# Three more seven-product blocks in the down projection of half 1, their weights loaded by rows, two banks seeded earlier, x reloaded after the last weight

## The chip, the cores and the metric

The kernel runs on 1 core of one Trainium2 chip. The metric is device time in microseconds (us); the kernel before takes 1061.85 us, the median of 3 runs (1061.6 to 1062.74). A core has TensorE (PE in the profile, with its weight load PEld), VectorE (DVE), ScalarE (ACT), GpSimd (POOL) and SyncE (SP), which here only issues DMAs. Each engine works through its own instructions in their order and waits where an operand, or the room for its result, isn't there yet.

## The reference, cut to what matters

One decoder layer on 256 tokens with 2048 channels, in float32. The part that the change touches is the end of its channel mixer:

```
u = causal_dwconv(h @ w_up, conv_w, conv_b)          # 256 x 11264
gate, val = split(u, 2)
y = (gelu(gate) * val) @ w_down                      # (256 x 5632) @ (5632 x 2048)
x = x + rmsnorm(y, post_ffn_g)
```

Attention, the input and output projections and the up projection come ahead of it and are computed as before.

## The kernel before, in words

**Products in float32.** Every weight is split into a high part (fp32r, by ACT: `whi`) and the rest (by DVE: `wlo = raw - whi`), and every activation likewise. A product is then three matmuls, high by high, high by low and low by high, into one PSUM bank (`products`, L973). A unit of weights is 128 partitions x 1024 numbers, 512 KB: SP loads it into one of 5 `raw` buffers (L72), ACT writes one of 5 `whi` buffers, DVE one of 5 `wlo` buffers.

**The down projection** runs in two halves of the 5632 rows. A half holds 22 row tiles of 128 in `G[0]` to `G[21]`, 256 tokens in two tiles t = 0 and 1, and makes two column pairs: n = 0 (columns 0 to 1023) and n = 2 (columns 1024 to 2047). For two row tiles, `four` (L1024) makes the products of one 512-column block with both tokens' tiles: 4 products of 512 columns, 12 matmuls. Two calls make the 8 products of a 2 x 2 x 2 block (row tiles x column blocks x token tiles).

**`seven`** (L988) makes those 8 products with 7, by Winograd's form of Strassen's scheme. Tokens' sums s1 to s4 come from POOL (L946 to L949) and are split into `sums`; weights' sums are made by DVE in place in the raw buffers (L1002 to L1005) and split as well. Of the 7 products, a, b and e (9 matmuls) come first, and d, f, c and g (12 matmuls, `others`, L1010) after the `four` calls of the same step, so that DVE has time for the sums. Seven splits of 512 columns and 4 subtractions are needed. The products a, c, d and f gather in four "att" banks over all sevens of the pair, and `fold` (L1031) then adds them to the four result blocks of y_sb: one ACT copy and 8 DVE additions in half 1. The table SEVENS (L28) says in which steps of a pair a seven stands: in half 0 at steps 0, 1, 3 and 4 of both pairs, in half 1 at steps 0, 2 and 4 of pair n = 0 and nowhere in pair n = 2.

**The last pair (half 1, n = 2; "the tail")** is made otherwise. The loop L1060 makes column block 2 alone (12 matmuls a step), and then L1115 makes column block 3: token tile 0 into bank e (6 matmuls of 512 columns for two row tiles), token tile 1 into two banks b1 in halves of 256 columns (12 matmuls of 256). For the last 6 pairs of row tiles (HOLD) the products of token tile 1 are put off to the end (`held`), so that token tile 0 can be normalised while PE still works. The banks b1 don't start from zero: at L1111 to L1114 a matmul opens each, and ACT copies into it what y_sb already holds for that block. PE's next product into b1 waits for this copy.

**Around it.** At a pair's end `down` (L963) adds a bank to y_sb (DVE), sums its squares (ACT, L967) and multiplies with post_ffn_g (POOL); for pair n = 0 of half 1 the four multiplications are listed in `gains` and are issued in the tail's loop (L1074). At the very end `finish` (L1105) multiplies with the reciprocal norm, adds x and stores. x was put aside in `x_dram`; it comes back into `x_end` (L1131), in the buffer in which `sums` stood. PE's order is the order of the code; the orders of DVE, ACT, POOL and SP are set by a scheduler when the kernel is built.

## Time and profile before

The profiled execution took 1063.41 us by the same clock as the runs and has a span of 1061.7 us; the runs without a profile have a median of 1061.85 us. A profile's busy time of an engine is the time in which an instruction of it runs; instructions of one engine overlap a little, so a group's count times its mean can be more.

| stretch of the trace (us from the start) | what runs | length | PE busy | DVE busy | ACT busy | POOL busy |
|---|---|---|---|---|---|---|
| 577.4 to 634.6 | half 0, pair 0 (four sevens) | 57.2 | 57.20 | 49.75 | 32.88 | 1.69 |
| 634.6 to 691.7 | half 0, pair 2 (four sevens) | 57.1 | 57.04 | 48.77 | 31.43 | 0.00 |
| 932.7 to 990.6 | half 1, pair 0 (three sevens) | 57.9 | 57.90 | 48.59 | 32.88 | 2.47 |
| 990.6 to 1020.5 | tail, column block 2 | 29.9 | 29.90 | 16.94 | 14.87 | 6.67 |
| 1020.5 to 1036.9 | tail, column block 3, both token tiles | 16.4 | 14.99 | 9.47 | 7.29 | 3.55 |
| 1036.9 to 1045.1 | tail, token tile 0 alone | 8.2 | 8.20 | 0.00 | 0.00 | 0.00 |
| 1045.1 to 1061.7 | held products, norm, stores | 16.6 | 8.62 | 7.51 | 1.67 | 2.35 |

In a row of a timeline the columns are the start, the duration, the engine, the line, the operation, result<-operands, shapes and count, and in brackets the engine's idle time ahead of it with what ended it.

### The profile page before, as it was taken

The numbers are of one execution on the slowest core, as the hardware profiler recorded it, in microseconds if no ns is written. First come the engines' busy times: TensorE is split into PE (matmuls) and PEld (weight loads), VectorE is DVE, ScalarE is ACT, GpSimd is POOL, SyncE is SP. The second block draws the span as 40 slices with busy tenths as digits, with TensorE's granted clock in tenths as the row PEclk, the third lists the DMA queues.
The fourth block names the chain that finished last, engine by engine and source line by source line (L and its number), as shares of the span: only waits on it lengthen the run. The fifth ranks groups of instructions, "written<-read, shape, count | busy, mean of one in ns | idle before, by whom it ended". The sixth has DMA issues, their size and how long they took to land.

```text
span 1061.7 us, 16409 instructions
## 1 busy us (share of the span) xinstructions
PE 1050.2 (99%) x5941; PEld 914.6 (86%) x5941; DVE 803.8 (76%) x1330; ACT 634.0 (60%) x1119; POOL 252.1 (24%) x278
## 2 busy tenths in 40 slices
PE   9999999999999999999999999999999999999996
PEld 7889988888889888888888888888888888888886
DVE  5989877876468787777768888868786777787653
ACT  6767766677557666655556555556565556555450
POOL 4253235441122433312111000013321212100210
PEclk9999999999999999999999999999999999999999
DMA  8645665555875766666664666866576656557742
GB/s 279 204 120 169 179 204 189 180 158 160 297 237 178 226 201 197 200 189 201 185 195 139 209 207 196 251 194 192 179 211 192 193 181 199 175 162 267 270 154 80
DMA packets 165550, 207.10 MB, mean 195 GB/s; under 512 B 6844, under 2 KB 131036, under 8 KB 164444
## 3 DMA queue, kind: packets, MB, share of 16 engines
q1 hardware_dynamic: 165148, 205.65, 61.9%
q8 instruction: 47, 0.77, 0.3%
q10 hardware_dynamic: 320, 0.40, 0.1%
q14 instruction: 35, 0.29, 0.1%
HBM read 201.68 MB, written 4.21 MB: 194 GB/s over the span
## 4 chain that ended last, share of the span: by engine, by line
PE 90%; DVE 4%; DMA 2%; issue 2%; ACT 1%; POOL 0%; SPq 0%; DVEq 0%; POOLq 0%; ACTq 0%
PE bank_acc L262 21%; PE bank_att L262 15%; PE bank_acc L975 13%; PE bank_acc L284 13%; PE bank_acc L269 11%; PE bank_att L269 8%; DMA raw<-in_w_down_dram 2%; PE bank_att L975 2%; DVE wlo L121 1%; PE bank_att L450 1%; PE bank_att L485 1%; PE bank_att L494 1%; DVE wlo L288 1%; PE bank_att L225 1%; PE bank_acc L881 1%
## 5 line engine op out<-in xcount | busy, mean ns | idle before, releaser
L121 DVE TENSOR_TENSOR wlo<-raw,whi 128x1024 fp32r<-128x1024 f32 (+3 forms) x335 | 408.7, 1233 | 140.4 <-ACT whi L118 133.5
L118 ACT CAST whi<-raw 128x1024 fp32r<-128x1024 f32 (+3 forms) x334 | 340.8, 1035 | 196.7 <-issue 90.7
L262 PE MATMUL bank_acc<-hT,whi 128*128 128x512 f32 x1024 | 245.6, 392 | 0.0
L262 PEld LDWEIGHTS bank_acc<-hT,whi 128*128 128x128 f32 x1024 | 188.2, 188 | 37.1
L857 POOL TENSOR_TENSOR u<-u,rowf 128x256 f32<-128x256 f32 x88 | 94.5, 1095 | 447.3 <-DVE u L856 444.3
L975 PE MATMUL bank_acc<-whi,G 128*128 128x512 f32 x520 | 167.6, 389 | 0.1
L262 PE MATMUL bank_att<-hT,whi 128*128 128x512 f32 x704 | 165.7, 390 | 0.0
L262 PEld LDWEIGHTS bank_att<-hT,whi 128*128 128x128 f32 x704 | 130.6, 188 | 26.2
L269 PEld LDWEIGHTS bank_acc<-hT,wlo 128*128 128x128 f32 x1024 | 123.5, 188 | 3.2
L269 PE MATMUL bank_acc<-hT,wlo 128*128 128x256 f32 x1024 | 125.8, 278 | 0.0
L975 PEld LDWEIGHTS bank_acc<-whi,G 128*128 128x128 f32 x520 | 97.6, 188 | 20.3 <-DVE y_sb L965 0.5
L975 PE MATMUL bank_acc<-wlo,G 128*128 128x512 f32 x260 | 101.2, 389 | 0.0
L269 PEld LDWEIGHTS bank_att<-hT,wlo 128*128 128x128 f32 x704 | 83.6, 188 | 1.9
L269 PE MATMUL bank_att<-hT,wlo 128*128 128x256 f32 x704 | 83.9, 277 | 0.0
L284 PE MATMUL bank_acc<-whi,oT 128*128 128x512 f32 (+1 forms) x272 | 81.8, 379 | 0.0
L287 ACT CAST whi<-raw 128x512 fp32r<-128x512 f32 x77 | 44.4, 621 | 27.2 <-DMA raw<-in_w_down_dram 14.5
L288 DVE TENSOR_TENSOR wlo<-raw,whi 128x512 fp32r<-128x512 f32 x77 | 52.7, 727 | 9.9 <-ACT whi L287 9.8
L284 PEld LDWEIGHTS bank_acc<-whi,oT 128*128 128x128 f32 x272 | 50.2, 188 | 9.3
L975 PEld LDWEIGHTS bank_acc<-wlo,G 128*128 128x128 f32 x260 | 48.8, 188 | 9.8
L284 PE MATMUL bank_acc<-wlo,oT 128*128 128x512 f32 (+1 forms) x136 | 51.2, 377 | 0.0
L284 PE MATMUL bank_acc<-whi,hT 128*128 128x384 f32 (+1 forms) x192 | 46.9, 323 | 0.0
L859 ACT ACTIVATE yg<-u,cw 128x256 f32<-128x256 f32 x44 | 26.5, 603 | 33.7 <-POOL u L857 33.7
(250 smaller groups left out, 1284.4 us busy)
## 6 DMA issues: line engine op xcount, KB each, us to landing
raw<-in_w_up_dram SPq DMA_DIRECT2D x176, 512.0 KB, 4.5
raw<-in_w_down_dram SPq DMA_DIRECT2D x88, 512.0 KB, 4.9
raw<-in_w_in_dram SPq DMA_DIRECT2D x51, 512.0 KB, 4.9
raw<-in_w_out_dram SPq DMA_DIRECT2D x32, 512.0 KB, 4.7
raw<-in_w_in_dram SPq DMA_DIRECT2D x16, 384.0 KB, 3.3
cb<-c_dram SPq DMA_DIRECT2D x8, 256.0 KB, 4.2
x_sb<-in_x_dram SPq DMA_DIRECT2D x2, 1024.0 KB, 6.0
x_dram<-x_sb SPq DMA_DIRECT2D x2, 1024.0 KB, 5.9
```

Source lines behind the costliest of these rows:

```text
L118: i1 = act.copy(hi[:, cs], raw[:, cs])
L121: i2 = dve.tensor_tensor(lo[:, cs], raw[:, cs], hi[:, cs].bitcast(F32), op=ALU.subtract)
L225: pe.matmul(b, hi[:, a, m * P:(m + 1) * P], hT[:, kt, 0:512], start=(kt == 0), stop=(kt == KT - 1))
L262: pe.matmul(b, hi[:, a, m * P:(m + 1) * P], hT[:, kt, 0:512], start=(kt == 0), stop=(last == (0, kt)))
L269: pe.matmul(b[:, 256:512], lo[:, a, m * P:(m + 1) * P], hT[:, u * 4 + a, 0:256], start=False, stop=(last == (1, u * 4 + a)))
L284: pe.matmul(b, a, r[:, cols], start=(first and i == 0), stop=(last and i == 2))
L287: act.copy(hi, src)
L288: dve.tensor_tensor(lo, src, hi.bitcast(F32), op=ALU.subtract)
L450: pe.matmul(sb[e][:, cs], a[r, t * P:(t + 1) * P], b[r, 0:nk], start=(n == 0), stop=(n == 2))
L857: pool.tensor_tensor(u[:, 2:258], u[:, 2:258], rowf, op=ALU.mult)
L859: act.activation(y, u[:, 2:258], AF.Identity, bias=cw[:, 3, ch:ch + 1], scale=cw[:, 2, ch:ch + 1])
L975: pe.matmul(b, x, r, start=b not in opened and not i, stop=closes and i == 2)
```

## The change

1. SEVENS for half 1 becomes (0, 1, 3, 4) in pair 0, so a fourth seven, and (0, 2) in the tail, which had none. The tail's loop then has 9 steps instead of 11, and the loop of column block 3 starts at the third pair of row tiles.
2. `seven` loads its weights by rows: two loads of 128 x 1024 (row tiles k and k + 1, both column blocks) instead of two of 2 x 128 x 512 (one column block each). `split_into` replaces `split_512`: the splits are one of 512 columns and three of 1024 instead of seven of 512. This holds for all sevens, half 0 too.
3. The banks b1 are opened and filled in the tail's loop, after step 6 (two steps before its end), instead of behind it.
4. The two reloads of x stay at their place in the program, which is behind the last weight's load; before, the scheduler put them among the weights. Their buffer is that of `sums`, which the tail now reads in its step 2.

```diff
-SEVENS = (((0, 1, 3, 4), (0, 1, 3, 4)), ((0, 2, 4), ()))
+SEVENS = (((0, 1, 3, 4), (0, 1, 3, 4)), ((0, 1, 3, 4), (0, 2)))
...
-            def split_512(dst, i, src):
-                cs = slice(i * 512, i * 512 + 512)
-                hi, lo = dst[0][:, cs], dst[1][:, cs]
-                split(hi, lo, src)
-                return hi, lo
+            def split_into(dst, src, n):
+                hi, lo = (x[:, :n * 512] for x in dst)
+                split(hi, lo, src[:, :n * 512])
+                return [(hi[:, i:i + 512], lo[:, i:i + 512]) for i in range(0, n * 512, 512)]
...
-                left, right = [w_load(w_rows(w_down, k, 2, m * 512, 512), 2, 512)[0]
-                               for m in (n, n + 1)]
-                b11, b21, b12, b22 = (x[:, i * 512:i * 512 + 512] for x in (left, right)
-                                      for i in range(2))
+                top, low = [w_load(w_rows(w_down, k + i, 1, n * 512, 1024), 1, 1024)[0]
+                            for i in range(2)]
+                b11, b12, b21, b22 = (x[:, i:i + 512] for x in (top, low) for i in (0, 512))
...
-                dst = w_parts(UNIT, held=False)
-                w11 = split_512(dst, 0, b11)
-                w22 = split_512(dst, 1, b22)
-                w21 = split_512(w_parts(UNIT, held=False), 0, b21)
+                (w11,) = split_into(w_parts(UNIT, held=False), top, 1)
+                w21, w22 = split_into(w_parts(UNIT, held=False), low, 2)
...
-                    dst = w_parts(UNIT, held=False)
-                    t1 = split_512(dst, 0, b11)
-                    t3 = split_512(dst, 1, b12)
-                    dst = w_parts(UNIT, held=False)
-                    t2 = split_512(dst, 0, b22)
-                    t4 = split_512(dst, 1, b21)
+                    t1, t3 = split_into(w_parts(UNIT, held=False), top, 2)
+                    t4, t2 = split_into(w_parts(UNIT, held=False), low, 2)
...
+                    if tail and i == (at[-1] + 4 if at else 0):
+                        b1 = [bank("att"), bank("att")]
+                        for x, cs in zip(b1, halves):
+                            pe.matmul(x[:, cs], G[0][:, 0:P], G[0][:, 0:256], start=True,
+                                      stop=False)
+                            act.copy(x[:, cs], y_sb[:, 1, 1536:2048][:, cs])
...
-        b1 = [bank("att"), bank("att")]
-        for x, cs in zip(b1, halves):
-            pe.matmul(x[:, cs], G[0][:, 0:P], G[0][:, 0:256], start=True, stop=False)
-            act.copy(x[:, cs], y_sb[:, 1, 1536:2048][:, cs])
...
-            sp.dma_start(x_sb[:, t, :], x_dram[t * P:(t + 1) * P, :])
+            i = sp.dma_start(x_sb[:, t, :], x_dram[t * P:(t + 1) * P, :])
+            if at:
+                tc.keep_in_program_order(i)
```

**Three places of the new order.** On DVE, at the passage from pair 0 of half 1 to the tail, the kernel before has this piece. `bank_acc` with L965 is a `down`, L121 the low part of a `four`'s weights:

```order
L1051 TENSOR_TENSOR y_sb<-y_sb,s 128x512
L121 TENSOR_TENSOR wlo<-raw,whi 128x1024 x2
L965 TENSOR_TENSOR y_sb<-bank_acc,y_sb 128x512 x2
L121 TENSOR_TENSOR wlo<-raw,whi 128x1024
L965 TENSOR_TENSOR y_sb<-bank_acc,y_sb 128x512 x2
L121 TENSOR_TENSOR wlo<-raw,whi 128x1024 x10
```

The changed kernel has this at the same place, where L998 to L1001 are the subtractions of a seven and L288 its low parts:

```order
L965 TENSOR_TENSOR y_sb<-bank_acc,y_sb 128x512 x2
L1000 TENSOR_TENSOR raw<-raw 128x512
L121 TENSOR_TENSOR wlo<-raw,whi 128x1024
L965 TENSOR_TENSOR y_sb<-bank_acc,y_sb 128x512 x2
L1001 TENSOR_TENSOR raw<-raw 128x512
L288 TENSOR_TENSOR wlo<-raw,whi 128x1024 x2
L121 TENSOR_TENSOR wlo<-raw,whi 128x1024
L288 TENSOR_TENSOR wlo<-raw,whi 128x512
```

The tail's first low part of a `four` now stands behind the first two `down` additions, and the two low parts of `others` (the pair of L288 rows) behind all four.

On PE, the kernel before opens the banks b1 (L1113) between the last product of column block 2 and the first of column block 3 (`G_7487` and `G_7488` are the last two row tiles of the half, `G_7467` the first):

```order
L975 MATMUL bank_acc<-whi,G_7488 128x512 x2
L975 MATMUL bank_acc<-wlo,G_7488 128x512
L975 MATMUL bank_acc<-whi,G_7488 128x512
L1113 MATMUL bank_att<-G_7467 128x256 x2
L975 MATMUL bank_acc<-whi,G_7467 128x512
L975 MATMUL bank_acc<-wlo,G_7467 128x512
L975 MATMUL bank_acc<-whi,G_7467 128x512
L284 MATMUL bank_att<-whi,G_7467 128x256
```

In the changed kernel the same two matmuls are L1070 and stand behind the row tiles 16 and 17 of the half (`G_7435` and `G_7436`):

```order
L975 MATMUL bank_acc<-whi,G_7436 128x512 x2
L975 MATMUL bank_acc<-wlo,G_7436 128x512
L975 MATMUL bank_acc<-whi,G_7436 128x512
L1070 MATMUL bank_att<-G_7419 128x256 x2
L975 MATMUL bank_acc<-whi,G_7437 128x512
L975 MATMUL bank_acc<-wlo,G_7437 128x512
```

Between the opening and the first product into b1 (L284) there are now 24 matmuls of column block 2, for row tiles 18 to 21, and 3 into bank e, where only those 3 stood.

On SP, the end of the changed kernel's queue reads:

```order
L72 DMA raw<-in_w_down_dram 128x1024 x2
L72 DMA raw<-in_w_down_dram 128x2x512 x2
L72 DMA raw<-in_w_down_dram 128x1024 x2
L72 DMA raw<-in_w_down_dram 128x2x512 x16
L1125 DMA x_end<-x_dram 128x2048 x2
L1106 DMA out_dram<-y_sb 128x512 x6
```

Both reloads of x (L1125) stand behind all weights; before, 21 and 15 weights were behind the first and the second.

## The prediction

> **What bounds the kernel now.** I read the page first, then busy time by stretches, then the chain of waits at the end of the span, then the timelines of the engines there. From the page:
>
> ```profile
> PE 1050.2 (99%) x5941; PEld 914.6 (86%) x5941; DVE 803.8 (76%) x1330; ACT 634.0 (60%) x1119; POOL 252.1 (24%) x278
> PE   9999999999999999999999999999999999999996
> PEclk9999999999999999999999999999999999999999
> ```
>
> PE is busy for all but the last slice, at its full clock. So a matmul that goes away is time that goes away, as long as the other engines keep ahead of PE; and the only other thing to win is a gap in PE's row. The stretches of the down projection (us, then PE, PEld, DVE, ACT, POOL with counts, clock, DMA share, GB/s):
>
> ```profile
> 577.40:634.60 57.20, 57.20 (x254) 47.36 (x253) 49.75 (x73) 32.88 (x49) 1.69 (x2) 1.00 0.60 195
> 932.70:990.60 57.90, 57.90 (x258) 47.92 (x257) 48.59 (x66) 32.88 (x47) 2.47 (x3) 1.00 0.69 229
> 990.60:1020.50 29.90, 29.90 (x133) 24.76 (x132) 16.94 (x15) 14.87 (x17) 6.67 (x4) 1.00 0.72 242
> 1020.50:1036.90 16.40, 14.99 (x94) 13.13 (x93) 9.47 (x10) 7.29 (x12) 3.55 (x2) 1.00 0.30 106
> ```
>
> The first row is a pair with four sevens, the second the pair with three, then the tail's column block 2 and the part of column block 3 with both token tiles. PE has a gap in the last one only, where the banks b1 are filled. DVE is the engine to watch: 87% busy with four sevens, 57% in the tail as it is.
>
> **Matmuls removed.** The pieces of the chain (start, us, what):
>
> ```profile
> 949.27 6.80 PE bank_acc L975 x30
> ...
> 1026.34 0.71 PE bank_att L284 x6
> 1027.05 0.69 PE bank_acc L975 x3
> ```
>
> A matmul of 512 columns costs 6.80 / 30 = 0.227 us. In column block 3 one row tile costs 0.69 + 0.71 = 1.40 us.
>
> - Pair 0 goes from 3 x 21 + 8 x 24 = 255 matmuls to 4 x 21 + 7 x 24 = 252: 3 x 0.227 = 0.68 us less. The two rows of stretches above say the same by themselves: 57.90 - 57.20 = 0.70. I take 0.70.
> - The tail's loop goes from 11 x 12 = 132 matmuls to 2 x 21 + 9 x 12 = 150: 18 x 0.227 = 4.08 us more. The loop of column block 3 loses 2 pairs, 4 row tiles: 4 x 1.40 = 5.60 less. Net 1.52 less.
>
> **The seeds of b1.** PE, and ACT's two copies, in the timeline:
>
> ```profile
> 1021.21 0.39 PE L975 MATMUL bank_acc<-whi,G 128*128 128x512 f32 x1
> ...
> 1022.28 0.36 ACT L1114 COPY bank_att<-y_sb 128x256 f32<-128x256 f32 x1
> ...
> 1022.70 0.38 PE L284 MATMUL bank_att<-whi,G 128*128 128x256 f32 x1 [1.10 <-ACT bank_att L1114]
> ...
> 1022.92 0.28 PE L284 MATMUL bank_att<-wlo,G 128*128 128x256 f32 x1
> ...
> 1023.04 0.28 PE L284 MATMUL bank_att<-whi,G 128*128 128x256 f32 x1
> ...
> 1023.62 0.39 PE L284 MATMUL bank_att<-whi,G 128*128 128x256 f32 x1 [0.31 <-ACT bank_att L1114]
> ...
> 1023.84 0.28 PE L284 MATMUL bank_att<-wlo,G 128*128 128x256 f32 x1
> ```
>
> A 256-column matmul costs 0.12 (0.71 / 6). Without the wait the matmul at 1022.70 would start at 1021.21 + 0.23 = 1021.44: 1.26 lost. That at 1023.62 would start at 1023.04 + 0.12: 0.46 lost. Each first one has its follower 0.22 later instead of 0.12: 0.20 lost. Together 1.92 us; the bracketed idle times alone (1.10 + 0.31 = 1.41) are the lower bound, since PE's ends are drawn later than its next start. In the changed order the copies have 24 matmuls of block 2 and 3 into e, 27 x 0.227 = 6.1 us, for two copies of 0.36. They need the tail's fold in y_sb, which has steps 3 to 6 (4 x 12 x 0.227 = 10.9 us) for 8 DVE additions of 0.6. So all 1.92 go. Were the cover gone, they would come back as they are.
>
> **What the sevens put on DVE and ACT.** One split and the subtractions, by the raw buffers' rows (min/median/max ns), and DVE's timeline:
>
> ```profile
> L121 DVE TENSOR_TENSOR wlo<-raw,whi x13: 1216/1220/1226, 954.7 to 989.2; 128x1024 fp32r<-128x1024 f32 x13
> L118 ACT CAST whi<-raw x12: 1045/1056/1060, 961.1 to 988.1; 128x1024 fp32r<-128x1024 f32 x12
> L287 ACT CAST whi<-raw x7: 615/622/625, 956.1 to 966.4; 128x512 fp32r<-128x512 f32 x7
> L288 DVE TENSOR_TENSOR wlo<-raw,whi x7: 683/685/693, 956.8 to 968.9; 128x512 fp32r<-128x512 f32 x7
> ...
> 964.73 0.68 DVE L1005 TENSOR_TENSOR raw<-raw 128x512 f32<-128x512 f32 x1
> 965.33 1.22 DVE L121 TENSOR_TENSOR wlo<-raw,whi 128x1024 fp32r<-128x1024 f32 x1
> 966.47 1.29 DVE L288 TENSOR_TENSOR wlo<-raw,whi 128x512 fp32r<-128x512 f32 x2
> ```
>
> Starts on a full DVE are 0.60 apart for 512 columns and 1.14 for 1024. By rows, a seven's splits take 0.62 + 3 x 1.06 = 3.80 of ACT instead of 7 x 0.62 = 4.34, and 0.60 + 3 x 1.14 = 4.02 of DVE instead of 4.20: a little less, in all sevens. PE waits in no pair with sevens now, so this is worth 0 in half 0 and in pair 0, whose new pattern is that of half 0, with DVE at 49.75 of 57.20. Its cover is those 7 us of free DVE. The added sums of half 1 (4 POOL instructions, two splits) run under the up projection, as three such sets do in the same half at a full PE.
>
> **The passage into the tail** is where something can be late. Let T be the tail's first matmul. DVE's queue there is in the order piece: two `down`, a subtraction, the first `four`'s low part, two `down`, a subtraction, then the two low parts of `others`. The first two `down` wait for banks that PE closes 12 matmuls ahead of T, so DVE starts at about T - 2.6. Then: 2 x 0.60, 0.72 (it depends on the instruction ahead), 1.14, which gives T + 0.46; the fourth `down` waits for PE's last matmul of the pair and ends by T + 1.65; 0.60, and 1.14 + 1.14 bring the low parts to T + 3.4 and T + 4.5. PE needs the first at T + (21 + 1) x 0.227 = 4.99, the second at T + 28 x 0.227 = 6.35. So 1.6 and 1.85 us are spare, without POOL. In the second seven the loads and the fold come in as well, but PE's 12 matmuls of step 1 stand between.
>
> POOL's four multiplications of `gains` start as soon as each block's squares are summed, just here:
>
> ```profile
> L1074 POOL TENSOR_TENSOR y_sb<-y_sb,gbc_ffn x4: 1302/1998/2281, 989.8 to 995.0; 128x512 f32<-128x512 f32 x4
> ...
> 990.29 1.28 DVE L965 TENSOR_TENSOR y_sb<-bank_acc,y_sb 128x512 f32<-128x512 f32 x2
> 991.87 2.00 DVE L121 TENSOR_TENSOR wlo<-raw,whi 128x1024 fp32r<-128x1024 f32 x1 [0.30 <-ACT whi L118]
> 994.59 1.52 DVE L121 TENSOR_TENSOR wlo<-raw,whi 128x1024 fp32r<-128x1024 f32 x1 [0.72 <-ACT whi L118]
> 997.31 1.22 DVE L121 TENSOR_TENSOR wlo<-raw,whi 128x1024 fp32r<-128x1024 f32 x1 [1.20 <-ACT whi L118]
> ...
> 989.82 7.45 POOL L1074 TENSOR_TENSOR y_sb<-y_sb,gbc_ffn 128x512 f32<-128x512 f32 x4 [54.19 <-ACT junk L967]
> ```
>
> A multiplication takes 1.30 alone and up to 2.28; beside it a low part of DVE takes 2.00 or 1.52 instead of 1.22, while the two `down` at 990.29, which read a PSUM bank, keep their 1.28 for two. So POOL and DVE's instructions with both operands in SBUF take turns. Today this costs nothing, for DVE is half idle there. In the changed queue DVE has five such instructions from T - 1.4 to the second low part, and each can find POOL ahead of it. If two of the four multiplications get in, DVE loses 2 x 1.30 = 2.6; if all four do, 5.2 less what runs beside the two `down` (2 x 0.60), so 4.0. Less the spare 1.85, PE waits 0.75 to 2.15 us at the third product of `others`. I take 1.0, near the lower end, because the rows show some multiplications finding DVE waiting; both ends are kept for the range.
>
> The Trainium skill's page "SBUF — State Buffer", section "Who interferes with whom", says the shared port is an exclusive lock which a VectorE instruction with two SBUF inputs and a GpSimd instruction that reads SBUF hold for their whole length, and that PE and ACT never wait for it. The 2.00 and 1.52 agree, and so do the undisturbed `down`; by a plain sharing of bandwidth there would be no wait and the sum would be 1.0 better.
>
> **x.** The issues, the transfer of the same size, and the first reader:
>
> ```profile
> x_dram<-x_sb SPq DMA_DIRECT2D x2, 1024.0 KB, 5.9
> ...
> 986.44 0.46 SPq L1131 DMA_DIRECT2D x_end<-x_dram  x1
> 987.69 35.34 SPq L72 DMA_DIRECT2D raw<-in_w_down_dram  x15
> ...
> 1048.54 2.74 DVE L1106 SCALAR_TENSOR_TENSOR y_sb<-y_sb,ry,x_end 128x512 f32<-128x512 f32 x4 [1.71 <-POOL ry L1095]
> ```
>
> Behind the last weight (987.69 + 35.34 = 1023.0) two transfers of 5.9 land by 1035, ahead of a reader at 1048.5 - 3: 10 us of cover, 0 cost. Behind them on SP stand only the stores. Two MB fewer then pass among the tail's first weights.
>
> **Sum**, against the profiled execution's span of 1061.7: -0.70 - 1.52 - 1.92 + 1.0 = -3.14, so 1058.6 for the span. The runs' median lies 0.15 above that span (the profiled execution's own time, 1063.41, has the profiler's cost in it), so 1058.7. What follows column block 3 (1045.1 to the end) has the same instructions and moves along. A change under 0.2% (2.1 us) can't be told from none here: faster means below 1059.7.
>
> **Rivals.**
>
> 1. *Full gain*: POOL's multiplications miss DVE's busy moments, nothing waits: -4.14, 1057.7. For it: the order in which POOL and DVE meet is known only to some tenths of a us, and the tail's weights come sooner without x among them. Against it: the four squares end exactly in this stretch. Chance 0.17.
> 2. *The taking of turns costs its most*: all four multiplications stand ahead of the low parts with nothing beside them, 5.2 - 1.85 = 3.35 of wait: 1061.85 - 4.14 + 3.35 = 1061.1, no measurable change. This is the lock of the Trainium skill's SBUF page taken whole. Chance 0.14.
> 3. *Late weights make it slower.* Between the sevens a load lands later than elsewhere:
>
> ```profile
> raw<-in_w_down_dram SPq DMA_DIRECT2D x88, 512.0 KB, 4.9
> ...
> DMA to landing us min/median/max: 5.3/6.4/7.1
> ```
>
> The first row is the page's median, the second that of the raw buffers from 955 to 990. A seven holds two of the five raw buffers until its second splits are done, so the load for the `four` of step 2 can be issued only at about T + 4.6. PE needs its low part at T + 12.5. With 4.9 for the load, 1.06 for ACT and 1.22 for DVE it is there at 11.8; with 7.1 at 14.0, 1.5 late, and three subtractions and two low parts stand behind it in DVE's order, 1.5 late in turn, so that the next loads are issued later and pay again. Three rounds of 1.5 and 2.15 from POOL give +6.7, 1064.4. It decides from a landing of about 5.7 us on. Against it: x is gone from this stretch and its loads come singly. Chance 0.06.
> 4. *The seeds still wait* since the fold or the copies are late: 1058.7 + 1.92 = 1060.6. Chance 0.03.
>
> The forecast, with a wait of 0.4 to 2.2 us, has 0.60. Faster: nearly all of the forecast (0.57), rival 1 (0.17) and a little of the rest: 0.76. Same: 0.17. Slower: 0.07. The range, 1057.4 to 1061.2, takes in rivals 1, 2 and 4.
>
> **What would show it.** Right: 252 matmuls in pair 0 of half 1 and 57.2 us for it; no gap of PE at b1; one gap of PE some 5 to 7 us into the tail, with DVE's L288 named as its end and beside POOL's L1066 of about 2.3; b1's copies done 4 us ahead of use; from the last product into e to the end 16.6 us as before. Wrong: a gap of PE in half 0; gaps all along the tail that end at a DMA; DVE's L1104 waiting for x.

## The result and the profile after

The changed kernel takes 1058.19 us, the median of 7 runs (1057.95 to 1058.76); the kernel before, beside it, 1061.6 (7 runs, 1061.4 to 1062.74). The ratio is 0.9968, with a 95% interval of 0.9958 to 0.9978: 3.4 us faster. A second set of runs gave 1058.15 (6 runs, 1057.9 to 1058.69) and 0.9968 again. The prediction was 1058.7.

Of the profile after, the page's first part, and then its busy time by stretches (length, then PE, PEld, DVE, ACT, POOL, clock, DMA share, GB/s): half 0, half 1's pair 0, the tail's column block 2, and half 1 from its first product to PE's end:

```profile
PE 1046.5 (99%) x5920; PEld 910.4 (86%) x5920; DVE 820.8 (78%) x1324; ACT 635.5 (60%) x1094; POOL 259.0 (25%) x282
```

```profile
575.75:690.00 114.25, 114.25 (x505) 94.60 (x505) 98.41 (x114) 62.11 (x68) 2.22 (x2) 1.00 0.65 210
930.70:987.85 57.15, 57.15 (x254) 47.31 (x253) 51.06 (x65) 33.27 (x41) 2.91 (x3) 1.00 0.60 194
987.85:1022.60 34.75, 34.27 (x150) 27.46 (x149) 32.74 (x34) 19.35 (x24) 9.36 (x4) 1.00 0.66 214
930.70:1048.85 118.15, 117.66 (x567) 98.46 (x565) 96.76 (x116) 59.89 (x78) 18.10 (x10) 1.00 0.59 196
```

The same two stretches of the kernel before, half 0 and half 1 to PE's end:

```profile
577.45:692.10 114.65, 114.59 (x505) 94.53 (x504) 98.87 (x137) 64.32 (x91) 1.69 (x2) 1.00 0.66 210
932.75:1053.75 121.00, 119.56 (x588) 100.95 (x586) 79.09 (x98) 56.23 (x79) 14.48 (x10) 1.00 0.57 192
```

The gain is in half 1: 588 matmuls became 567, and 121.0 us became 118.15. DVE is busy for 32.74 of the 34.75 us of the tail's column block 2; before, it was 16.94 of 29.90.

The span fell by 4.9 us (1061.7 to 1056.8), more than the time. The rest lies at the very start. Two pieces of PE's timeline, of before and then of the changed kernel, for the same work:

```profile
6.50 1.11 PE L309 MATMUL bank_acc<-ident,x_in 128*128 128x128 f32 x4 [0.39 <-DMA x_in<-in_x_dram]
7.27 2.05 PE L225 MATMUL bank_att<-hT,whi 128*128 128x512 f32 x4
9.12 1.05 PE L230 MATMUL bank_att<-hT,wlo 128*128 128x256 f32 x4
```

```profile
5.96 0.66 PE L309 MATMUL bank_acc<-ident,x_in 128*128 128x128 f32 x4
6.37 1.18 PE L225 MATMUL bank_att<-hT,whi 128*128 128x512 f32 x4
7.39 0.63 PE L230 MATMUL bank_att<-hT,wlo 128*128 128x256 f32 x4
```

In the profiled execution of before the first projection was 1.73 us late (9.12 - 7.39), and everything behind it kept that. A load of x that landed late explains 0.54 of it (6.50 against 5.96). The rest is PE's pace: four matmuls of 512 columns take 2.05 us there and 1.18 in the changed kernel. The trace's record of PE's granted clock begins only at 10.64 us in that execution, and between 4.7 and 6.8 in every other profile, so a clock granted late is the likely reason; no run tests it. The change touches nothing there. So single executions differ by up to 2 us at their start, and what a change does inside is better read from the length of a stretch.

**Stretches of all runs.** Half 0 is from the down projection's first product to the up projection's next one; half 1 is from its first product to the end of PE's last matmul. A gap is the time between two matmuls' starts beyond the usual 0.23 us; counted so, the wait at b1 comes out 0.3 under the prediction's 1.92, which goes by the pace of 256 columns. "Rows" and "columns" is how the sevens' weights are loaded. The stretch between the halves takes 240.7 us in every run, and from PE's end to the span's end all take 7.9 to 8.0; what stands ahead of half 0 takes 575.6 to 577.5. Each ratio is against runs of the kernel before made beside that run (medians 1061.54 to 1061.84).

| run | weights | half 0 | half 1 | gaps in half 1 | median (lowest to highest, runs) | ratio, 95% |
|---|---|---|---|---|---|---|
| before | columns | 114.62 | 120.93 | 1.62 at b1 | 1061.6 (1061.4 to 1062.74, 7) | |
| changed | rows | 114.24 | 118.13 | 1.26 in the tail's loop | 1058.19 (1057.95 to 1058.76, 7) | 0.9968, 0.9958 to 0.9978 |
| changed, again | rows | 114.24 | 117.65 | 0.80 in the loop | 1058.15 (1057.9 to 1058.69, 6) | 0.9968, 0.9957 to 0.998 |
| multiplications last | rows | 114.24 | 116.78 | none | 1057.25 (1057.01 to 1057.52, 5) | 0.9957, 0.9944 to 0.9969 |
| multiplications doubled | rows | 114.24 | 121.96 | in the loop | 1062.5 (1062.27 to 1062.99, 10) | 1.0009, 0.9999 to 1.0018 |
| no sevens in the tail | rows | 114.24 | 118.33 | none | 1058.88 (1058.68 to 1059.68, 9) | 0.9976, 0.9966 to 0.9986 |
| rows only | rows | 114.24 | 121.05 | 1.74 at b1 | 1061.66 (1061.19 to 1062.58, 11) | 1.0001, 0.9992 to 1.001 |
| seeds only | columns | 114.24 | 119.01 | none | 1059.69 (1059.29 to 1060.21, 11) | 0.9981, 0.9972 to 0.999 |
| fourth seven only | columns | 114.29 | 121.36 | 1.07 at the passage, 1.61 at b1 | 1061.4 (1060.35 to 1062.42, 11) | 0.9998, 0.9989 to 1.0007 |
| x free | rows | 114.24 | 118.02 | 0.99, some at b1 | 1059.39 (1058.14 to 1059.88, 9) | 0.9975, 0.9965 to 0.9985 |
| changed, by columns | columns | 114.24 | 117.62 | 0.77 in the loop | 1060.04 (1058.11 to 1062.09, 11) | 0.9985, 0.9976 to 0.9994 |
| the same, again | columns | 114.74 | 119.50 | 2.6, from the passage on | 1060.15 (1057.95 to 1062.04, 11) | 0.9979, 0.997 to 0.9988 |
| by columns, multiplications last | columns | 114.24 | 116.78 | none | 1057.22 (1056.97 to 1057.92, 5) | 0.996, 0.9948 to 0.9973 |
| third seven in the tail | rows | 114.24 | 118.67 | 2.56 at b1 | 1059.92 (1058.07 to 1060.29, 9) | 0.9978, 0.9968 to 0.9987 |

**Where PE waits now.** The timelines of PE, DVE and POOL in the changed kernel, behind the tail's first matmul at T = 987.85:

```profile
996.12 0.50 PE L975 MATMUL bank_acc<-wlo,G 128*128 128x512 f32 x1 [0.42 <-DVE wlo L121]
```

```profile
985.64 1.28 DVE L965 TENSOR_TENSOR y_sb<-bank_acc,y_sb 128x512 f32<-128x512 f32 x2
...
988.57 1.28 DVE L965 TENSOR_TENSOR y_sb<-bank_acc,y_sb 128x512 f32<-128x512 f32 x2
...
990.37 1.22 DVE L288 TENSOR_TENSOR wlo<-raw,whi 128x1024 fp32r<-128x1024 f32 x1
991.80 2.03 DVE L288 TENSOR_TENSOR wlo<-raw,whi 128x1024 fp32r<-128x1024 f32 x1 [0.21 <-ACT whi L287]
993.75 2.31 DVE L121 TENSOR_TENSOR wlo<-raw,whi 128x1024 fp32r<-128x1024 f32 x1
995.99 2.91 DVE L288 TENSOR_TENSOR wlo<-raw,whi 128x512 fp32r<-128x512 f32 x2
```

```profile
987.16 10.05 POOL L1066 TENSOR_TENSOR y_sb<-y_sb,gbc_ffn 128x512 f32<-128x512 f32 x4 [53.07 <-ACT junk L967]
```

POOL's four multiplications last 10.05 us where four alone need 5.2, and beside them DVE's low parts take 2.03 and 2.31 instead of 1.22. The two pairs of `down` additions, one operand of which is in PSUM, keep their 1.28, the second of them beside POOL. PE stops where the low part made at 993.75 is used: the `four` of step 1, behind the first seven. It loses 0.68 us there (0.57 and then 0.11). Smaller gaps follow in the second seven (0.13 + 0.11 at 1003.5, 0.24 + 0.10 at 1005.1), 0.58 together. At b1 PE doesn't wait; ACT's two copies, and PE's first product into b1:

```profile
1022.56 0.67 ACT L1072 COPY bank_att<-y_sb 128x256 f32<-128x256 f32 x2
```

```profile
1024.12 0.28 PE L284 MATMUL bank_att<-whi,G 128*128 128x256 f32 x1
```

### The profile page after: what moved, and what is told of

It is laid out like the page before. It is cut to its first block, busy times and chain, and to the rows that moved or that the text cites. A ratio compares the mean times of both kernels' runs of the same rounds, so it can differ in the third digit from the quotient of the medians.

```text
span 1056.8 us, 16351 instructions
## 1 busy us (share of the span) xinstructions
PE 1046.5 (99%) x5920; PEld 910.4 (86%) x5920; DVE 820.8 (78%) x1324; ACT 635.5 (60%) x1094; POOL 259.0 (25%) x282
## 4 chain that ended last, share of the span: by engine, by line
PE 89%; DVE 4%; DMA 2%; issue 2%; ACT 1%; POOL 0%; SPq 0%; DVEq 0%; POOLq 0%; ACTq 0%
PE bank_acc L262 21%; PE bank_att L262 15%; PE bank_acc L284 13%; PE bank_acc L975 12%; PE bank_acc L269 11%; PE bank_att L269 7%; PE bank_att L975 2%; DMA raw<-in_w_down_dram 2%; DVE wlo L121 1%; PE bank_att L450 1%; PE bank_att L485 1%; PE bank_att L494 1%; DVE wlo L288 1%; PE bank_acc L881 1%; PE bank_acc L225 1%
## 5 line engine op out<-in xcount | busy, mean ns | idle before, releaser
L121 DVE TENSOR_TENSOR wlo<-raw,whi 128x1024 fp32r<-128x1024 f32 (+3 forms) x329 | 400.6, 1231 | 121.5 <-ACT whi L118 114.3
L118 ACT CAST whi<-raw 128x1024 fp32r<-128x1024 f32 (+3 forms) x328 | 333.5, 1033 | 174.6 <-issue 84.5
L975 PE MATMUL bank_acc<-whi,G 128*128 128x512 f32 x492 | 159.5, 389 | 0.0
L975 PEld LDWEIGHTS bank_acc<-whi,G 128*128 128x128 f32 x492 | 92.4, 188 | 19.0
L975 PE MATMUL bank_acc<-wlo,G 128*128 128x512 f32 x246 | 95.9, 390 | 0.4 <-DVE wlo L121 0.4
L284 PE MATMUL bank_acc<-whi,oT 128*128 128x512 f32 (+1 forms) x272 | 81.8, 379 | 0.0
L287 ACT CAST whi<-raw 128x1024 fp32r<-128x1024 f32 (+1 forms) x56 | 51.7, 942 | 35.2 <-PE bank_acc L975 15.9
L288 DVE TENSOR_TENSOR wlo<-raw,whi 128x1024 fp32r<-128x1024 f32 (+1 forms) x56 | 62.2, 1133 | 6.5 <-ACT whi L287 6.5
L284 PEld LDWEIGHTS bank_acc<-whi,oT 128*128 128x128 f32 x272 | 50.2, 188 | 9.3
L975 PEld LDWEIGHTS bank_acc<-wlo,G 128*128 128x128 f32 x246 | 46.2, 188 | 10.2 <-DVE wlo L121 0.8
L284 PE MATMUL bank_acc<-wlo,oT 128*128 128x512 f32 (+1 forms) x136 | 51.2, 377 | 0.0
L284 PE MATMUL bank_acc<-whi,hT 128*128 128x384 f32 (+1 forms) x192 | 46.9, 323 | 0.0
```

The source lines that it names most:

```text
L118: i1 = act.copy(hi[:, cs], raw[:, cs])
L121: i2 = dve.tensor_tensor(lo[:, cs], raw[:, cs], hi[:, cs].bitcast(F32), op=ALU.subtract)
L284: pe.matmul(b, a, r[:, cols], start=(first and i == 0), stop=(last and i == 2))
L287: act.copy(hi, src)
L288: dve.tensor_tensor(lo, src, hi.bitcast(F32), op=ALU.subtract)
L975: pe.matmul(b, x, r, start=b not in opened and not i, stop=closes and i == 2)
```

## The experiments

The theory to test: POOL's multiplications and DVE's low parts take turns at the passage into the tail, and that alone stands between the changed kernel and the full sum of its parts. The rivals are that late weights cause the gaps, and that the parts aren't worth what the sum says.

**The multiplications last.**

```diff
-                sp.dma_start(gbf, post_ffn_g[0].partition_broadcast(P))
+                sp.dma_start(gbf[:, 1024:], post_ffn_g[0][1024:].partition_broadcast(P))
...
-                    if i == max((0, *at)):
-                        for args, kw in gains:
-                            pool.tensor_tensor(*args, **kw)
...
+        tc.keep_in_program_order(
+            sp.dma_start(gbf[:, :1024], post_ffn_g[0][:1024].partition_broadcast(P)))
+        for args, kw in gains:
+            pool.tensor_tensor(*args, **kw)
```

> The changed kernel, with POOL's four multiplications of pair 0 held back until the tail's sevens are done: the part of post_ffn_g that they read is loaded behind the last weight. DVE's order is the same row for row. Theory P (the tail's gaps in PE's row, 1.27 us in all by the spacing of its matmuls, come from POOL and DVE taking turns): no spacing over 0.29 us in the tail, DVE's low parts there back at 1.22 instead of 2.03 and 2.31, span from the first down product of half 1 to PE's end 1.0 to 1.3 shorter than the 118.13 us of the changed kernel, time about 1057.0 us where before takes 1061.6. Theory W (late weights): gaps as in the changed kernel, 1058.2 us.

The busy time of half 1 in this run, then DVE's and POOL's timelines:

```profile
931.05:1047.90 116.85, 116.83 (x567) 98.70 (x566) 93.07 (x116) 60.44 (x78) 12.52 (x10) 1.00 0.62 203
```

```profile
990.26 1.23 DVE L288 TENSOR_TENSOR wlo<-raw,whi 128x1024 fp32r<-128x1024 f32 x1
991.71 1.23 DVE L288 TENSOR_TENSOR wlo<-raw,whi 128x1024 fp32r<-128x1024 f32 x1 [0.22 <-ACT whi L287]
992.85 1.22 DVE L121 TENSOR_TENSOR wlo<-raw,whi 128x1024 fp32r<-128x1024 f32 x1
993.98 1.82 DVE L288 TENSOR_TENSOR wlo<-raw,whi 128x512 fp32r<-128x512 f32 x2
```

```profile
1028.22 1.30 POOL L1123 TENSOR_TENSOR y_sb<-y_sb,gbc_ffn 128x512 f32<-128x512 f32 x1 [93.75 <-DMA gbc_ffn<-in_post_ffn_g_dram]
```

The same DVE instructions now take 1.23, 1.23, 1.22 and 1.82: with T = 988.22 here, the low part of step 1's `four` is done at T + 5.85 instead of T + 8.22, 2.37 us sooner. Of the 2.37, 0.5 isn't POOL's: DVE's first `down` addition stands 2.7 us ahead of T here and 2.2 in the changed kernel's first profile (the changed kernel again, below, has 2.7 as well). No gap is left. Half 1 takes 116.78, which is 120.93 - 4.15: the prediction's full sum was 4.14. This version is faster than both kernels, 1057.25 us.

**The multiplications doubled.** Only POOL's order differs from the changed kernel's.

```diff
-                        for args, kw in gains:
+                        for args, kw in gains * 2:
```

> The changed kernel with each of the four POOL multiplications of `gains` issued twice, eight in all at the same place; DVE's, ACT's, PE's and SP's orders are as in the changed kernel. The second gain makes columns 0 to 1023 of the sum before the norm differ from the layer's; this output is left wrong. Theory (POOL and DVE take turns, and PE pays what is over DVE's spare time): the second four last until about 1006, into the second seven and behind it; each takes up to 1.3 us from DVE, 5.2 in all, and with the spare already used up by the first four 3 to 5 us of it reach PE: from the down projection's second half to PE's end 121 to 123 us instead of 118.1, time 1061 to 1063. Rival (the 1.35 us that the moved multiplications won came from something else, such as the halved load of the gains): 118.1 as in the changed kernel, time 1058.2.

PE's waits from 570 to 1040, then POOL's and DVE's timelines:

```profile
PE bank_acc L975 <- DVE wlo L121: 2.2, 1, 2.2
PE bank_acc L975 <- DVE wlo L288: 0.2, 1, 0.2
```

```profile
987.25 17.39 POOL L1066 TENSOR_TENSOR y_sb<-y_sb,gbc_ffn 128x512 f32<-128x512 f32 x8 [53.02 <-ACT junk L967]
```

```profile
993.38 2.31 DVE L121 TENSOR_TENSOR wlo<-raw,whi 128x1024 fp32r<-128x1024 f32 x1
995.61 4.00 DVE L288 TENSOR_TENSOR wlo<-raw,whi 128x512 fp32r<-128x512 f32 x2
999.54 1.77 DVE L998 TENSOR_TENSOR raw<-raw 128x512 f32<-128x512 f32 x1
1001.23 2.28 DVE L121 TENSOR_TENSOR wlo<-raw,whi 128x1024 fp32r<-128x1024 f32 x1
```

POOL goes on for 17.4 us and DVE's instructions stay long as far as it goes: a subtraction of 512 columns takes 1.77 instead of 0.68. Half 1 takes 121.96. With none, four and eight multiplications in the tail it is 116.78, then 118.13 and 117.65, then 121.96: the first four cost 0.87 to 1.35, the second four 3.8 to 4.3 of the 5.2 that four last alone. The spare time hides part of the first four and little of the second. Nothing but POOL's list was changed, so this and the run before settle that the multiplications cause the gaps. The rows also tell turns from a plain sharing of bandwidth, which would lengthen a long instruction more than a short one (the prediction had said that sharing would bring no wait at all): a subtraction of 512 columns grows by 1.09 us (0.68 to 1.77), a low part of 1024 by just as much (1.22 to 2.31). By the Trainium skill, page "SBUF — State Buffer", section "Who interferes with whom", the shared port is an exclusive lock and the blocked engine stands still, which these rows bear out.

**No sevens in the tail**: pair 0's fourth seven, the rows and the early seeds stay (without sevens, the seeds go behind step 6).

```diff
-SEVENS = (((0, 1, 3, 4), (0, 1, 3, 4)), ((0, 1, 3, 4), (0, 2)))
+SEVENS = (((0, 1, 3, 4), (0, 1, 3, 4)), ((0, 1, 3, 4), ()))
...
-                    if tail and i == (at[-1] + 4 if at else 0):
+                    if tail and i == (at[-1] + 4 if at else 6):
```

> The changed kernel without its two sevens in the tail (b1 seeded behind step 6 all the same, x not pinned). By the sum it loses 1.52 us and the tail's gaps of 1.27 go: 1058.4 us, so the two sevens are worth 0.25 us as they stand. If the gaps have another cause than the sevens: 1059.7 us.

Half 1 takes 118.33 without a gap, so the tail's two sevens bring 0.2 to 0.7 as they stand, of their 1.52: the turns take the rest. With the multiplications last they bring 1.55 (118.33 - 116.78).

**One part alone**, three runs: the rows; the early seeds; pair 0's fourth seven. The first, on the kernel as changed, leaves sevens and seeds as they were before:

```diff
-SEVENS = (((0, 1, 3, 4), (0, 1, 3, 4)), ((0, 1, 3, 4), (0, 2)))
+SEVENS = (((0, 1, 3, 4), (0, 1, 3, 4)), ((0, 2, 4), ()))
```

> The kernel before with the sevens' weights loaded and split by rows, nothing else. The prediction's working has 0: 1061.6 us. By the two traces a gap of 0.34 us at the first seven of half 0's second pair goes: 1061.3 us.

The second keeps the columns and puts the seeds into the loop:

```diff
-        b1 = [bank("att"), bank("att")]
...
+                    if tail and i == 6:
+                        b1 = [bank("att"), bank("att")]
...
```

> The kernel before with the banks b1 opened and filled behind step 6 of the tail's loop, nothing else. The prediction's working: 1.92 us less, 1059.7 us. By the bracketed idle times alone: 1.41 less, 1060.2 us.

The third is the kernel before with one more seven:

```diff
-SEVENS = (((0, 1, 3, 4), (0, 1, 3, 4)), ((0, 2, 4), ()))
+SEVENS = (((0, 1, 3, 4), (0, 1, 3, 4)), ((0, 1, 3, 4), ()))
```

> The kernel before with a fourth seven in pair 0 of half 1 (steps 0, 1, 3, 4), nothing else. The prediction's working: 0.70 us less, 1060.9 us. If the two sevens on end at the passage from the up projection make PE wait: 1061.6 us or more.

Half 1's busy time with the rows alone, and with the seeds alone:

```profile
930.90:1051.95 121.05, 119.53 (x588) 100.99 (x586) 78.73 (x90) 55.34 (x71) 15.28 (x10) 1.00 0.58 192
```

```profile
930.95:1049.95 119.00, 119.00 (x588) 101.01 (x586) 80.39 (x98) 56.00 (x79) 14.90 (x10) 1.00 0.59 196
```

The rows alone are worth nothing (ratio 1.0001), the seeds alone 1.92 us (120.93 - 119.01), as forecast. The fourth seven alone wins its 0.70 and gives 1.07 back at the passage into the tail. The timelines of ACT, DVE and PE there:

```profile
986.57 1.05 ACT L118 CAST whi<-raw 128x1024 fp32r<-128x1024 f32 x1 [2.64 <-DMA raw<-in_w_down_dram]
```

```profile
988.27 1.28 DVE L965 TENSOR_TENSOR y_sb<-bank_acc,y_sb 128x512 f32<-128x512 f32 x2
```

```profile
989.10 0.47 PE L975 MATMUL bank_acc<-whi,G 128*128 128x512 f32 x1 [0.83 <-DVE y_sb L965]
```

ACT waited for a weight, DVE's `down` additions began at 988.27 instead of some 986, and PE waited for a bank. That execution (1062.1 us) is one of the slowest of the eleven; their median is 0.2 below the kernel before, not 0.7. With the rows the same seven kept its gain (no sevens in the tail against seeds only: 118.33 and 119.01, 0.68).

**The changed kernel by columns**, run twice. The splits and loads of `seven` are those of before:

```diff
-                top, low = [w_load(w_rows(w_down, k + i, 1, n * 512, 1024), 1, 1024)[0]
-                            for i in range(2)]
+                left, right = [w_load(w_rows(w_down, k, 2, m * 512, 512), 2, 512)[0]
+                               for m in (n, n + 1)]
...
-                    t1, t3 = split_into(w_parts(UNIT, held=False), top, 2)
-                    t4, t2 = split_into(w_parts(UNIT, held=False), low, 2)
+                    dst = w_parts(UNIT, held=False)
+                    t1 = split_512(dst, 0, b11)
...
```

> The changed kernel with its sevens' weights loaded and split by columns as before (seven splits of 512 instead of one of 512 and three of 1024). Theory P: DVE has 0.18 to 0.3 us more work a seven, so the tail's gaps grow by 0.2 to 0.6, and the gap of 0.34 us in half 0 (at 637 us in the kernel before, absent in the changed one) is back: 1058.7 to 1059.1 us. Theory W, by which the rows matter for the loads: 1059.5 us or more. If rows do nothing: 1058.2 us.

> The sevens' weights by columns with the multiplications of `gains` in the tail, a second time: its first eleven runs had a median of 1060.04 us but lay between 1058.11 and 1062.09, while its one trace had the second half of the down projection in 117.6 us. Theory A (columns bring seven low parts of 512 columns where rows bring one and three of 1024, more places where POOL can get in ahead of DVE, so the wait differs from run to run and is mostly over 1.3 us): the trace shows 118.5 to 120 us in the second half, with its gaps in the tail's sevens, and the median is again 1059.5 to 1060.5. Theory B (the first runs differed in their start, from the first loads): the trace shows 117.5 to 118.2 in the second half, and the median is 1058 to 1059.

The first profile is of the fastest of its eleven runs (1058.11): it had 117.62 in half 1, no more than with rows and without half 0's gap, against the expectation. The median of those runs, 1060.04, lies where theory W had it. The second profile caught an execution near the median (1060.43), with the 119.50 that theory A had expected. Its stretches of half 0 and half 1, its waits of SP and ACT in half 1's pair 0 (931 to 990), and DVE's first `down` additions:

```profile
575.80:690.55 114.75, 114.58 (x505) 94.53 (x505) 99.04 (x137) 64.19 (x91) 1.69 (x2) 1.00 0.67 210
931.25:1050.75 119.50, 117.85 (x567) 98.31 (x565) 97.89 (x133) 61.51 (x95) 17.68 (x10) 1.00 0.59 194
```

```profile
SPq L72 <- DVE wlo L288: 12.1, 7, 5.1
...
ACT whi L118 <- DMA raw<-in_w_down_dram: 6.7, 6, 2.4
ACT whi L287 <- DMA raw<-in_w_down_dram: 6.2, 4, 3.3
```

```profile
987.46 1.28 DVE L965 TENSOR_TENSOR y_sb<-bank_acc,y_sb 128x512 f32<-128x512 f32 x2
```

The same waits of the changed kernel, with rows, in its second profile:

```profile
SPq L72 <- DVE wlo L288: 8.4, 7, 2.6
...
ACT whi L118 <- DMA raw<-in_w_down_dram: 4.7, 4, 2.3
ACT whi L287 <- DMA raw<-in_w_down_dram: 1.1, 2, 0.6
```

By columns SP waits up to 5.1 us for a seven's low part before it may load into that raw buffer (in every profile by columns), by rows up to 2.6 (in every one by rows). ACT then waits 12.9 us for weights against 5.8. DVE comes to its `down` additions 0.9 us ahead of the tail's first matmul; with rows, in the changed kernel's two profiles, 2.2 and 2.7 ahead. POOL's turns do the rest: 2.6 us of gaps. Theory A's reason, more places for POOL to get in, doesn't hold: in both profiles by columns, as in both with rows, POOL lengthens three instructions of DVE (to 1.7 to 2.3 us). What differs is when DVE arrives.

SP's longer wait doesn't make an execution late by itself. The first profile by columns has the same 5.1, and there ACT waits only 5.4 us for weights and DVE is 2.8 ahead. That columns leave less room for a load that lands late is an argument from these figures, not shown. Why one execution by columns is on time and the next is late isn't settled: a load took 4.7 us (median of 22) from issue to landing in the first profile's pair 0 and 5.9 (of 21) in the second, but what makes them land late no run shows.

**By columns, with the multiplications last**, to see whether columns cost anything without POOL.

> The multiplications of `gains` at the end, as in the run that moved them, and the sevens' weights by columns as in the kernel before. Theory (POOL and DVE taking turns is the only wait of the tail, and the way the weights are loaded is worth nothing): no gap of PE in the second half, 116.8 us from its first product to PE's end, as with rows; time 1056.5 to 1058. Rival (columns cost DVE and ACT something that the tail has not to spare: 0.2 us of DVE and 0.5 of ACT for a seven): a gap at the second seven of the tail, 117.0 to 117.6.

116.78 in half 1 without a gap and 1057.22 us, the same as with rows (116.78 and 1057.25). DVE comes to its `down` additions only 1.3 us ahead of the tail here, and PE doesn't wait. So rows are worth 0 on the kernel before, 1.9 us by the medians (1060.1 - 1058.2; 1.2 and 1.8 by the ratios) beside POOL's multiplications, and 0 again once these are gone. The 1.9 is no fixed price: of the 22 runs by columns 17 are slower than the slowest of the 13 with rows (1058.76), and five are as fast. Rows change the loads and the splits together; which of the two counts isn't separated.

**x free**: the reloads of x where the scheduler puts them.

```diff
-            i = sp.dma_start(x_sb[:, t, :], x_dram[t * P:(t + 1) * P, :])
-            if at:
-                tc.keep_in_program_order(i)
+            sp.dma_start(x_sb[:, t, :], x_dram[t * P:(t + 1) * P, :])
```

> The changed kernel without the pin on the reloads of x: the scheduler puts the first four weights ahead of the end and the second at the end. The loads of the tail's sevens stand ahead of both, so theory P and theory W both expect no change of the gaps near the sevens: 1058.2 us, within 0.3. If x's transfer delays the last weights, a gap of PE at the end of block 3 and up to 2 us more.

Half 1 takes 118.02, inside the 117.65 to 118.13 of the changed kernel, with a small part of the gaps (0.29) now at b1. The runs' median is 1.2 higher (1059.39, against the 1058.2 expected), and this profile began 1.2 us later (first down product at 577.0 against 575.8; near its start PE waits 0.99 for a weight's cast), so what x costs, if anything, can't be told from the start's spread.

**The changed kernel again**, beside the two runs on POOL and columns.

> The changed kernel once more, in the same call as the two others. If the stretches of one profile stand for the kernel: 114.2 us for half 0 and 118.0 to 118.2 from half 1's first product to PE's end, with gaps at the first `four` behind the first seven and in the second seven; the start of the first product may differ by 1 to 2 us. If the 0.5 us between rows and columns is chance of one execution, the second stretch comes out between 117.5 and 118.5.

Its gaps have the same places and add up to 0.80 instead of 1.26: 0.19 at the `four` of step 1 and 0.61 in the second seven. The turns are the same, as DVE's rows show beside those of the first profile; T is 987.67 here:

```profile
984.98 1.28 DVE L965 TENSOR_TENSOR y_sb<-bank_acc,y_sb 128x512 f32<-128x512 f32 x2
...
991.15 2.02 DVE L288 TENSOR_TENSOR wlo<-raw,whi 128x1024 fp32r<-128x1024 f32 x1 [0.22 <-ACT whi L287]
993.09 2.31 DVE L121 TENSOR_TENSOR wlo<-raw,whi 128x1024 fp32r<-128x1024 f32 x1
```

What differs is when DVE arrives: its first `down` stands 2.7 us ahead of T instead of 2.2. In the first profile ACT had waited 1.38 us for a weight late in pair 0, and DVE 0.61 for ACT:

```profile
976.87 1.05 ACT L118 CAST whi<-raw 128x1024 fp32r<-128x1024 f32 x1 [1.38 <-DMA raw<-in_w_down_dram]
```

```profile
977.95 1.23 DVE L121 TENSOR_TENSOR wlo<-raw,whi 128x1024 fp32r<-128x1024 f32 x1 [0.61 <-ACT whi L118]
```

In the second profile the same cast waited 0.26 us, and DVE didn't wait for it. The profiles side by side show that a DVE up to 1.4 us later costs PE nothing without the multiplications, and with them nearly its whole delay:

| run | weights | multiplications at the passage | DVE's first `down` ahead of T | half 1 |
|---|---|---|---|---|
| changed, by columns | columns | four | 2.8 | 117.62 |
| changed, again | rows | four | 2.7 | 117.65 |
| changed | rows | four | 2.2 | 118.13 |
| changed, by columns, again | columns | four | 0.9 | 119.50 |
| multiplications last | rows | none | 2.7 | 116.78 |
| by columns, multiplications last | columns | none | 1.3 | 116.78 |

**A third seven in the tail**, with the multiplications last, in search of a still faster version.

```diff
-SEVENS = (((0, 1, 3, 4), (0, 1, 3, 4)), ((0, 1, 3, 4), (0, 2)))
+SEVENS = (((0, 1, 3, 4), (0, 1, 3, 4)), ((0, 1, 3, 4), (0, 2, 4)))
...
-                    if tail and i == (at[-1] + 4 if at else 0):
+                    if tail and i == (at[-1] + 3 if at else 0):
```

> As the run with POOL's multiplications held back, with a third seven in the tail (steps 0, 2 and 4). One tail seven is worth 9 matmuls more in the loop of block 2 (2.04 us) against 2 row tiles less in block 3 (2.80 us), so 0.76 us. Theory P, with DVE's 8.0 us of work a seven step against 7.5 of PE, and a step between: 1056.3 us if nothing waits, 1057.0 if the fold and the third seven's low parts, now closer together, eat the gain. Theory W: 1058.5 us or more, since the gaps multiply with the sevens.

The loop has no gap, but b1 has one of 2.56. DVE, ACT and PE:

```profile
1025.80 0.69 DVE L1043 TENSOR_TENSOR y_sb<-y_sb,s 128x512 f32<-128x512 f32 x1
```

```profile
1027.29 0.67 ACT L1069 COPY bank_att<-y_sb 128x256 f32<-128x256 f32 x2
```

```profile
1027.70 0.39 PE L284 MATMUL bank_att<-whi,G 128*128 128x256 f32 x1 [2.40 <-ACT bank_att L1069]
```

The fold's last addition stands behind the low parts of the next weights in DVE's order and comes at 1025.80, the copies at 1027.29; PE could have used b1 at 1025.15 (0.23 behind its product of 1024.92). The edit also opens b1 in the loop's last step (1024.21), but the fold's last addition ends later (1026.49), so it is the fold that holds b1 up, and ACT's other work ahead of the copies adds to it. The late fold that the prediction gave a small chance has a real price here, and the version loses to the one with two sevens.

## Why the prediction was right, step by step

- **Matmuls removed, -0.70 and -1.52**: right. Pair 0 takes 57.15 (forecast 57.2). With the multiplications out of the way all parts together come to 4.15 of the 4.14 reckoned: 1.92 for the seeds, 0.68 for the fourth seven, 1.55 for the tail's two.
- **The seeds, -1.92**: right to 0.01 with the seeds alone. Their cover was over-sized: the copies in the changed kernel ran from 1022.56 to 1023.23, 0.9 us ahead of the first product into b1 (1024.12) and not 4, since DVE strings the fold's eight additions out until 1019.1 (the prediction had them inside 10.9 us from 1003.7) and ACT's casts stand ahead of the copies. It cost nothing here, 2.56 with a third seven.
- **The passage, +1.0 for taking turns**: the mechanism is right, as removing and doubling the multiplications show; the size is 0.87 in one execution and 1.35 in the other, inside the bounds of 0.75 and 2.15. The place was wrong. The low parts of `others` were ready in time (the second one at T + 6.0, needed at T + 6.35); the first gap is at the `four` of step 1, whose low part is next in DVE's order. It has 1.86 us to spare (ready at T + 5.85 without POOL, needed at T + 7.71) and came 2.37 later than that in the first profile, 1.88 in the second. The order piece quoted ahead of the prediction has this row; the working stopped one row short of it. The rest of the wait (0.58 and 0.61) lies in the second seven, where the prediction put nothing because 12 matmuls stand between. By then three instructions of DVE have been lengthened by 3.0 us in all (2.03, 2.31 and 1.77), where the prediction's sum had two multiplications at 2.6. So the size came out by luck: the two spares happen to be equal, and what the second seven adds, which was left out, stays inside the bounds. DVE's start at T - 2.6, taken as given, held in the second profile and not in the first.
- **Rows at 0, with 7 us of free DVE as cover**: this step failed. Alone rows are worth nothing, as predicted; in the changed kernel they hold 1.9 of the 3.4 us by the medians, since beside the multiplications PE pays for a DVE that arrives late, and with rows it came 2.2 and 2.7 us ahead where by columns it could be 0.9. The free DVE time of a whole pair is no cover for that moment. The prediction costed the two edits apart and so missed their product. Why rows keep DVE early isn't settled; SP's shorter wait for a raw buffer (2.6 against 5.1) is a candidate.
- **"PE waits in no pair with sevens now"** was misread: in the profile of before PE has a gap of 0.34 in half 0's second pair, at 637 us. By columns half 0 takes 114.24 to 114.74, with rows 114.24 in every profile. It is too little to move the sum.
- **x at 0**: not contradicted, and not measured well either.
- **The sum's foot**: the prediction took the 1.6 us between the profiled execution's time and the runs' median for a cost of profiling. It is the late start of that one execution (1.73 us); in the others the time is 1.7 us over the span too (1058.56 for 1056.8). The sum was made against the median and so wasn't hurt. From the other executions' figures it reads 1061.6 - 4.14 + 0.87 to 1.35, which is 1058.3 to 1058.8; measured 1058.2.
- **Rivals**: the full gain (1057.7) is what the version with the multiplications last gave (1057.25). All turns at their most (1061.1) didn't come about with four multiplications. Of late weights, the rounds of later and later loads didn't come about. But a weight that came late made DVE late, and beside the multiplications that cost half 1 some 0.5 us with rows and 1.9 by columns; with the fourth seven alone, by columns, it stopped PE even ahead of them (1.07). The seeds' rival came true only with a third seven.

## What to carry to other kernels

Before an engine's free time is filled with work, see which of its instructions share a port with another engine there, and whether that other engine's work could be done later: on the changed kernel by columns, moving four multiplications is worth 2.9 us (1060.1 - 1057.2) and loading by rows 1.9. Follow the order of a filled engine past the instruction that seems critical to the next few, for a stall lands on the first one whose spare time is less than the delay. A part that is worth nothing alone can still carry half of a change's gain, so take it out of the whole as well as adding it alone.

## What the runs showed of the hardware

- DVE and POOL instructions with both operands in SBUF lengthen each other by about one instruction of the other engine: a split of 1.22 us takes 2.0 to 2.3, a subtraction of 0.68 takes 1.77, and a multiplication of 1.29 takes 2.5 on the mean (10.05 for four). Additions with a PSUM operand aren't touched (1.28 for two).
- The same order of instructions gave 0.80 and 1.26 us of gaps in two executions, with the same turns in both: a weight that landed later made DVE 0.5 us later in one.
- The start of a kernel varies: the down projection began between 575.6 and 577.5 us with the same work ahead of it. The latest had PE's matmuls at half their pace for the first microseconds (four of 512 columns in 2.05 us instead of 1.18).
